# Moving small constants and two attention pools so that matmul operands start at multiples of 512 bytes

## The chip, the cores and the metric

The kernel runs on one core of a Trainium2 chip. The metric is the device time of one execution in microseconds (us). The core has five engines that work side by side: TensorE (PE) multiplies, and its weight loads (PEld) are recorded separately; VectorE (DVE) and ScalarE (ACT) do elementwise work; GpSimd (POOL) does elementwise work between SBUF tiles; SyncE (SP) issues nearly all DMA transfers. SBUF is the working memory of 128 partitions; a tile takes the same byte range in every partition, and its start address below is the byte at which that range begins. PSUM takes the results of the matmuls.

## The reference, cut to what matters

One encoder layer (depth 1, so only mixer A), in float32, on 2048 tokens of width 1024:

```python
mod = (silu(c) @ ada_w + ada_b); sh1, sc1, g1, sh2, sc2, g2 = split(mod, 6)
h = rmsnorm(x, mix_norm_pre) * (1 + sc1) + sh1
y = windowed_gqa_sink(h, w_qkv, w_o, sink, rel_bias)   # 16 heads, 4 KV heads, window +-128
x = x + g1 * rmsnorm(y, mix_norm_post)
h = rmsnorm(x, ffn_norm_pre) * (1 + sc2) + sh2
y = (silu(a) * b) @ w_out, where a, b = split(h @ w_in, 2)   # hidden 2816
x = x + g2 * rmsnorm(y, ffn_norm_post)
```

## The kernel before, in words

**Number format.** A float32 product is made of three matmuls on rounded parts: `three` (lines 147 to 151) multiplies high weights by high activations (L149), high weights by low activations (L150) and low weights by high activations (L151). `split` (line 153) makes the parts: ACT copies the rounded high part (L154), DVE or POOL subtracts it (L155). Nearly every matmul has a stationary operand (the weights) of 128 x 128 values, 512 bytes per partition, and a moving operand of 128 x 512 values, 2048 bytes per partition. Each matmul is preceded by a load of its weights, which goes on while the matmul before it still streams.

**Stages.** (1) The projections of token chunks 0 and 1 (`Chunk`, `w_piece`, `qkv_tile`; matmuls `psq<-hi,w` and `psv`). (2) Attention, 64 units of 128 queries and one KV head each (`Unit`): `scores` (L432), transposes of the probabilities (L455), `values` (L460, L461). Between the units a `Budget` puts filler matmuls on PE: the projections of chunks 2 and 3 (`psq<-hi,ws`), later the output projection of chunks 0 to 2 (`py<-ol,wo`). (3) The output projection of chunk 3 (`last_o`, again `py<-ol,wo`), once attention has given its memory back. (4) The first FFN product (`Hidden`, `pc_i`) in two halves of 1024 tokens: for each of 22 output tiles seven block products (`Block.STEPS`) of 12 matmuls each. (5) The second product (`Outs`, `pc_o`): in seven parts of m = 2 or 3 pairs of hidden tiles (`PARTS`), four blocks per part, each of seven steps of 3 x m matmuls. (6) A last part without the block scheme (`pl`), and the final norm.

**Order.** The instructions of an engine run in a fixed order, which a scheduler works out when the program is built. SP's DMA issues are one such queue: an issue that waits holds up all behind it.

**Where tiles lie.** Tiles live in pools, and pools are stacks that grow from both ends of SBUF: `side="left"` upwards, `side="right"` downwards. A pool opened later lies further in; a pool's memory is used again once it is closed, and a new tile then waits for the last users of the old ones (`reuse_waits="tile"`). Sizes are rounded up to 32 bytes. So one tile of an odd size moves every pool that is opened behind it on that side:

- Left: 1152 bytes are taken before the kernel's first tile. `const` (lines 106 to 113) adds 192 + 192 + 128 + 64 + 512 + 512 + 32 + 128 = 1760 bytes, so the next pool starts at 2912 = 5 x 512 + 352. All left pools behind it hold tiles whose sizes are multiples of 512: each operand there starts 352 bytes past a multiple of 512. `ones` and `ident`, inside `const`, start at 192 past one.
- Right: the end is at 229,344 = 447 x 512 + 480. All right pools with tiles of whole multiples of 512 give operands at 480 past a multiple.
- In attention `sm` (eight tiles of 32 bytes) and `pp` (three tiles `pr` of 6176 bytes) take 18,784 bytes = 36 x 512 + 352, so the pools opened after them, `ptp`, `ob` and `ws` (lines 376 to 378), hold operands at 128 past a multiple.

Which operand comes from which side, with its start past a multiple of 512 ("offset"):

| Matmuls | moving operand | weights |
|---|---|---|
| `psq<-hi,w`, `psq<-lo,w` (stage 1) | `hs`, left, 352 | `w1`, `w2`, right, 480 |
| `psq<-hi,ws` (fillers) | `hs`, left, 352 | `ws`, right, 128 |
| `py<-ol,wo`, chunks 0 to 2 | `op`, left, 352 | `ws`, right, 128 |
| `o<-phi,v`, `o<-plo,v` | `ptp`, right, 128 | `v` in `qkv`, right, 480 |
| `s<-k,q` | `k` in `qkv`, right, 480 | `q` in `qkv`, right, 480 |
| `py<-ol,wo`, chunk 3 | `op3`, right, 480 | `wop3`, right, 480 |
| `pc_i`, steps 0 to 4 of 7 | left, 352 | even tiles `wi0`, left, 352; odd tiles `wi1`, right, 480 |
| `pc_i`, steps 5 and 6 | `hB`, right, 480 | the same |
| `pc_o`, two steps (`hb11o`, `ht2o`) | `hA2`, left, 352 | `wo`, left, 352 |
| `pc_o`, the other five steps | `hB2`, right, 480 | `wo`, left, 352 |
| `pl<-gls,wl` | half left, 352; half right, 480 | `hB2`, right, 480 |

**The hand-over after attention.** When `att` closes (line 682), `yp3`, `wop3` and `op3` (lines 688 to 690) are opened on the right, over attention's memory. `OProj.fill` loads four tiles `ol` (attention's output, L543) and, per output tile, a raw weight `wor` (L553), which ACT and DVE split into `wo`.

Of the kernel before, what the change touches and what calls it, by code (L numbers as in the profile page):

```python
# [11 lines left out]
F32 = mybir.dt.float32  # L12
# [6 lines left out]
P = 128  # L19
S = 2048  # L20
D = 1024
KT = D // P
# [25 lines left out]
LAG = 2  # L48
# [15 lines left out]
def f(ap):  # L64
    return ap.bitcast(F32)
# [8 lines left out]
def encoder_layer(ctx, tc, a):  # L74
# [4 lines left out]
    def open_pool(stack, name, bufs=1, side="left", space=None):  # L79
        kw = {"space": space} if space is not None else {"side": side}  # L80
        return stack.enter_context(tc.tile_pool(name=name, bufs=bufs, reuse_waits="tile", **kw) if space is not DRAM
                                   else tc.tile_pool(name=name, bufs=bufs, space=DRAM))

    const = open_pool(ctx, "const")
    dram = open_pool(ctx, "dram", space=DRAM)

    q_d = [[dram.tile([P, GRP, CH], F32, name=f"q_d{c}_{g}") for g in range(KVH)] for c in range(NCH)]
# [15 lines left out]
    tab_d = dram.tile([HEADS, RLEN], F32, name="tab_d")  # L103


    mod = const.tile([P, 48], F32, name="mod")
    adab = const.tile([P, 48], F32, name="adab")
    gains = const.tile([P, 4, KT], F32, name="gains")
    nsink = const.tile([P, HEADS], F32, name="nsink")
    ones = const.tile([P, P], F32R, name="ones")  # L110
    ident = const.tile([P, P], F32, name="ident")
    epsc = const.tile([P, 1], F32, name="epsc")
    coef = const.tile([P, 4, KT], F32, name="coef")
    dve.memset(f(ones), 1.0 / D)
    dve.memset(epsc, EPS)
    make_identity(nc, ident)
# [254 lines left out]
    att = ExitStack()  # L371
    bp = open_pool(att, "bp", side="right")
    qkv = open_pool(att, "qkv", 2, side="right")
    sm = open_pool(att, "sm", 4, side="right")
    pp = open_pool(att, "pp", LAG + 1, side="right")
    ptp = open_pool(att, "ptp", 4, side="right")
    ob = open_pool(att, "ob", 2, side="right")
    wop = ws = open_pool(att, "ws", 2, side="right")
    psF = open_pool(ctx, "psF", 2, space=PSUM)
    psS = open_pool(att, "psS", 2, space=PSUM)  # L380
    psT = open_pool(att, "psT", 3, space=PSUM)
# [751 lines left out]
```

## Time and profile before

| | |
|---|---|
| Median of 3 runs | 2166.03 us (2165.94 to 2170.61) |
| The profiled execution, first to last instruction | 2164.3 us |
| Instructions in it | 28,995, of them 9366 matmuls |
| ACT busy | 1076.4 us (50%) |
| POOL busy | 737.5 us (34%) |
| DMA moved | 396.35 MB, mean 183 GB/s |

A row of a view of the trace reads: start in us from the span's start, duration in us, engine, source line, operation, tile written <- tiles read, shape, and in brackets the idle time of the engine before it with what ended it. The end of a matmul is modelled and overlaps the next one; the distance from one start to the next is what PE takes per matmul, and that is what is read below. Tile names have their numbers left out.

### The profile page before, as it was taken

The page shows a single profiled execution, that of the slowest core. Times are in us where ns is not written, and L with a number is a line of the kernel's source. Part 1 is how long each engine was busy: PE and PEld are TensorE (multiplying, and loading weights), DVE is VectorE, ACT ScalarE, POOL GpSimd, SP SyncE. Part 2 cuts the span into 40 slices and gives each one's busy share as a digit, 9 for nine tenths or more (in the row PEclk, how much of TensorE's full clock was granted, in tenths as well). Part 3 has the DMA queues.
Part 4 walks back from the last instruction along what each step waited for, and adds up shares of the span by engine and source line. Part 5 has one row for each costly group of instructions (what it writes and reads, how often), then busy time and mean ns, then how long its engine had stood idle before and what let it go on. Part 6 is the DMA issues. An engine that isn't in the chain of part 4 may idle for free. (4 is left out here: it accounts for less than half of the span.)

```text
span 2164.3 us, 28995 instructions
## 1 busy us (share of the span) xinstructions
PE 2055.8 (95%) x9366; PEld 1666.6 (77%) x9366; DVE 1649.8 (76%) x2933; ACT 1076.4 (50%) x2125; POOL 737.5 (34%) x687
## 2 busy tenths in 40 slices
PE   6898999989989989999999999999999999998996
PEld 4786877878867768878887877888888788877886
DVE  7656767665676669876878897767673888999987
ACT  4546666577777746343434342333332844465422
POOL 3404343367778723434344422222221000220030
PEclk8999999999999989999999999999999999999998
DMA  8877665576667695545455764332231644438442
GB/s 279 261 254 253 184 182 175 159 282 233 227 199 245 189 347 206 183 148 162 138 178 194 257 220 142 112 106 94 98 117 54 210 153 138 141 129 280 161 132 103
DMA packets 200516, 396.35 MB, mean 183 GB/s; under 512 B 20091, under 2 KB 62124, under 8 KB 195244
## 3 DMA queue, kind: packets, MB, share of 16 engines
q1 hardware_dynamic: 199788, 393.97, 54.7%
q8 instruction: 74, 1.21, 0.2%
q14 instruction: 78, 0.64, 0.1%
q10 hardware_dynamic: 576, 0.52, 0.1%
HBM read 270.65 MB, written 123.76 MB: 182 GB/s over the span
## 5 line engine op out<-in xcount | busy, mean ns | idle before, releaser
L437 DVE CUSTOM_DVE_ANT_0 pr<-s,bias,nsink 128x384 f32<-128x384 f32 (+1 forms) x256 | 149.3, 596 | 91.5 <-PE s L432 74.3
L149 PE MATMUL pc_i<-ht,ws_i 128*128 128x512 f32 x528 | 207.2, 393 | 2.1 <-DVE b_i L799 1.5
L150 PE MATMUL pc_i<-ht,ws_i 128*128 128x512 f32 x528 | 206.9, 392 | 0.0
L151 PE MATMUL pc_i<-ht,ws_i 128*128 128x512 f32 x528 | 206.9, 392 | 0.0
L439 ACT ACTIVATE pr<-pr,nm 128x385 f32<-128x385 f32 (+1 forms) x256 | 153.8, 603 | 71.3 <-DVE nm L437 64.3
L815 POOL TENSOR_TENSOR p_i<-p_i,u_i 128x512 f32<-128x512 f32 x44 | 71.5, 1625 | 310.7 <-DVE u_i L802 153.6
L445 POOL TENSOR_SCALAR pr<-pr,rs 128x384 f32<-128x384 f32 (+1 forms) x256 | 147.4, 601 | 83.0 <-DVE rs L443 82.9
L946 POOL TENSOR_TENSOR z<-z,z 128x512 f32<-128x512 f32 x32 | 52.5, 1654 | 359.2 <-DVE z L942 342.3
L432 PE MATMUL s<-k,q 128*128 128x384 f32 (+1 forms) x512 | 136.1, 359 | 20.2 <-DVE nm L437 13.6
L149 PE MATMUL pc_i<-hb,wa_i 128*128 128x512 f32 x352 | 139.1, 395 | 2.0 <-DVE u_i L789 2.0
L150 PE MATMUL pc_i<-hb,wa_i 128*128 128x512 f32 x352 | 138.7, 394 | 0.0
L151 PE MATMUL pc_i<-hb,wa_i 128*128 128x512 f32 x352 | 138.7, 394 | 0.0
L155 DVE TENSOR_TENSOR plo<-t,phi 128x512 fp32r<-128x512 f32 x184 | 121.7, 685 | 16.2 <-ACT phi L154 14.7
L154 ACT CAST wa_i<-wiri 128x512 fp32r<-128x512 f32 x132 | 81.8, 620 | 102.2 <-PE pc_i L151 94.7
L154 ACT CAST ws_i<-s_i 128x512 fp32r<-128x512 f32 x132 | 81.6, 618 | 102.5 <-PE pc_i L151 98.7
L432 PEld LDWEIGHTS s<-k,q 128*128 128x128 f32 x512 | 86.6, 193 | 44.9 <-DVE nm L437 27.8
L149 PEld LDWEIGHTS pc_i<-ht,ws_i 128*128 128x128 f32 x528 | 99.3, 188 | 25.5 <-DVE b_i L799 2.2
L151 PEld LDWEIGHTS pc_i<-ht,ws_i 128*128 128x128 f32 x528 | 99.2, 188 | 22.4
L150 PEld LDWEIGHTS pc_i<-ht,ws_i 128*128 128x128 f32 x528 | 99.2, 188 | 22.2
L455 PE MATMUL t<-ident,pr 128*128 128x128 f32 x736 | 113.1, 273 | 3.1 <-POOL pr L445 2.4
L149 PE MATMUL py<-ol,wo 128*128 128x512 f32 x256 | 103.3, 405 | 11.9 <-ACT wo L154 7.4
L155 DVE TENSOR_TENSOR ws_i<-s_i,ws_i 128x512 fp32r<-128x512 f32 x132 | 104.6, 792 | 10.9 <-ACT ws_i L154 10.7
(320 smaller groups left out, 6142.8 us busy)
## 6 DMA issues: line engine op xcount, KB each, us to landing
wiri<-w_in SPq DMA_DIRECT2D x88, 512.0 KB, 4.8
ada<-ada_w SPq DMA_DIRECT2D x40, 512.0 KB, 4.9
wiro<-w_out SPq DMA_DIRECT2D x48, 384.0 KB, 3.9
q_d<-e SPq DMA_DIRECT2D x64, 256.0 KB, 3.9
q<-q_d SPq DMA_DIRECT2D x16, 1024.0 KB, 5.8
wo<-wo_d SPq DMA_DIRECT2D x16, 1024.0 KB, 5.7
g_d_b<-p_i SPq DMA_DIRECT2D x44, 256.0 KB, 4.7
g_d_t<-p_i SPq DMA_DIRECT2D x40, 256.0 KB, 2.0
```

The lines of the kernel that those rows point to most:

```text
L149: pe.matmul(ps, w[0], h[0], start=first, stop=False)
L150: pe.matmul(ps, w[0], h[1], start=False, stop=False)
L151: pe.matmul(ps, w[1], h[0], start=False, stop=last)
L154: act.copy(hi, src)
L155: return eng.tensor_tensor(lo, src, f(hi), ALU.subtract).ins
L432: m = pe.matmul(ps[:, :n], q[:, h, jb * P:(jb + 1) * P], kk[:, i, (jb + j0) * P:(jb + j1) * P], start=i == 0, stop=i == 1)
L437: red = dve.tensor_tensor_reduce(pr[:, h, :n], ps[:, :n], bias[g][:, h, j0 * P:j1 * P], -1.0, nsink[:, hh:hh + 1], ALU.add, ALU.min, nm[:, ...
L439: act.activation(pr[:, h, :n + 1], pr[:, h, :n + 1], AF.Exp, bias=nm[:, h:h + 1], scale=-1.0, accum_out=rs[:, h:h + 1])
L445: pool.tensor_scalar(pr[:, h, :n], pr[:, h, :n], rs[:, h:h + 1], 1.0, ALU.mult, ALU.mult)
L455: pe.transpose(pt[:, h * P:(h + 1) * P], pr[:, h, jj * P:(jj + 1) * P], ident)
L815: pool.tensor_tensor(sa, sa, b, ALU.mult)
L946: (pool if (i, x) in ((2, 2), (4, 4), (5, 5), (6, 6)) else dve).tensor_tensor(sums[hf, n2, x], sums[hf, n2, x], sums[hf, n2, y], ALU.add)
```

## The change

It moves tiles and pools; it adds, removes and resizes no operation. `mod` is declared with 80 columns instead of 48, of which 48 are used as before. `adab`, `gains`, `epsc` and `coef` go to a new pool `constr` at the right end: 192 + 128 + 32 + 128 = 480 bytes, so the right pools now start at 228,864 = 447 x 512. On the left `const` is 320 + 64 + 512 + 512 = 1408 bytes; `ones` starts at 1536, `ident` at 2048 and the next pool at 2560, all multiples of 512. In attention `sm` and `pp` are opened last, behind `ptp`, `ob` and `ws`. The one matmul operand that stays off a multiple of 512 is `pr` in the transposes (L455), whose rows are 385 values wide.

```diff
     const = open_pool(ctx, "const")
+    constr = open_pool(ctx, "constr", side="right")
     dram = open_pool(ctx, "dram", space=DRAM)
...
-    mod = const.tile([P, 48], F32, name="mod")
-    adab = const.tile([P, 48], F32, name="adab")
-    gains = const.tile([P, 4, KT], F32, name="gains")
+    mod = const.tile([P, 80], F32, name="mod")
+    adab = constr.tile([P, 48], F32, name="adab")
+    gains = constr.tile([P, 4, KT], F32, name="gains")
     nsink = const.tile([P, HEADS], F32, name="nsink")
     ones = const.tile([P, P], F32R, name="ones")
     ident = const.tile([P, P], F32, name="ident")
-    epsc = const.tile([P, 1], F32, name="epsc")
-    coef = const.tile([P, 4, KT], F32, name="coef")
+    epsc = constr.tile([P, 1], F32, name="epsc")
+    coef = constr.tile([P, 4, KT], F32, name="coef")
...
     qkv = open_pool(att, "qkv", 2, side="right")
-    sm = open_pool(att, "sm", 4, side="right")
-    pp = open_pool(att, "pp", LAG + 1, side="right")
     ptp = open_pool(att, "ptp", 4, side="right")
     ob = open_pool(att, "ob", 2, side="right")
     wop = ws = open_pool(att, "ws", 2, side="right")
+    sm = open_pool(att, "sm", 4, side="right")
+    pp = open_pool(att, "pp", LAG + 1, side="right")
```

In the built program the order of instructions is the same on every engine up to the hand-over after attention. There SP's queue differs: before, it issues `ol` 0 early, then `ol` 1, `ol` 2, `wor` 0, `ol` 3, `wor` 1, `wor` 2; after, `wor` 0 takes the early place, then come `wor` 1, 2, 3 and behind them `ol` 0 to 3. Some instructions of ACT, DVE and PE in this stretch and in the first blocks of `pc_i` change places with it.

## The prediction

> **What bounds the kernel now.** I read the page first, then busy time by stage, then PE's waits.
>
> ```profile
> span 2164.3 us, 28995 instructions
> PE 2055.8 (95%) x9366; PEld 1666.6 (77%) x9366; DVE 1649.8 (76%) x2933; ACT 1076.4 (50%) x2125; POOL 737.5 (34%) x687
> PEclk8999999999999989999999999999999999999998
> ```
> ```profile
> 0.00:182.00 182.00, 150.13 (x684) 120.32 (x684) 118.26 (x179) 86.21 (x145) 47.22 (x34) 0.93 0.80 263
> 182.00:756.00 574.00, 545.67 (x2770) 443.02 (x2770) 385.80 (x991) 404.49 (x931) 341.50 (x430) 0.99 0.65 210
> 756.00:822.00 66.00, 55.18 (x221) 44.44 (x222) 44.41 (x56) 35.60 (x56) 17.42 (x9) 0.90 0.97 354
> 822.00:1690.00 868.00, 858.10 (x3709) 697.11 (x3708) 671.45 (x956) 321.49 (x547) 277.40 (x183) 1.00 0.44 148
> 1690.00:2098.00 408.00, 396.69 (x1678) 317.32 (x1677) 378.78 (x651) 210.52 (x411) 50.39 (x31) 0.98 0.51 169
> 2098.00:2164.00 66.00, 49.99 (x309) 44.37 (x307) 51.09 (x102) 18.11 (x38) 3.60 (x3) 0.91 0.32 108
> ```
>
> The columns are the stretch, its length, busy time of PE, PEld, DVE, ACT and POOL, granted clock, DMA share, GB/s. PE has work in 858 of 868 us of `pc_i`, 397 of 408 us of `pc_o` and 546 of 574 us of attention, mostly at full clock. A busy PE here is a queue of matmuls: what a stretch costs is their number times the distance between two starts. PE hardly waits:
>
> ```profile
> PE s L432 <- DVE nm L437: 13.3, 20, 2.0
> PE nstl L131 <- DVE nhil L129: 5.5, 2, 4.0
> PE pc_o L149 <- DVE z L942: 6.5, 1, 6.5
> PE psq L149 <- ACT hi L154: 12.5, 3, 8.5
> ```
>
> These are the longest waits of attention, of `pc_i`, of `pc_o` and of the projections (total us, times, longest). So the question is only whether addresses alter the distance between starts.
>
> **They do already.** Two neighbouring blocks of `pc_i`, an even and an odd output tile, same line numbers and shapes, first and last row of each run without a gap:
>
> ```profile
> 1610.91 0.39 PE L149 MATMUL pc_i<-hb,wa_i 128*128 128x512 f32 x1
> ...
> 1624.29 0.39 PE L151 MATMUL pc_i<-ht,ws_i 128*128 128x512 f32 x1
> 1624.52 0.40 PE L149 MATMUL pc_i<-ht,wa_i 128*128 128x512 f32 x1
> ...
> 1629.88 0.39 PE L151 MATMUL pc_i<-hb,ws_i 128*128 128x512 f32 x1
> 1630.11 0.40 PE L149 MATMUL pc_i<-hb,wa_i 128*128 128x512 f32 x1
> ...
> 1643.88 0.39 PE L151 MATMUL pc_i<-ht,ws_i 128*128 128x512 f32 x1
> 1644.10 0.39 PE L149 MATMUL pc_i<-ht,wa_i 128*128 128x512 f32 x1
> ...
> 1649.33 0.40 PE L151 MATMUL pc_i<-hb,ws_i 128*128 128x512 f32 x1
> ```
>
> The runs have 60, 24, 60 and 24 rows, so the distances are 13.38/59 = 226.8 ns (moving and weights both at offset 352), 5.36/23 = 233.0 (480 and 352), 13.77/59 = 233.4 (352 and 480), 5.23/23 = 227.4 (both 480). Equal offsets: 227. Unequal: 233. The output projection shows it under one name, chunk 2 (352 and 128) and chunk 3 (both 480):
>
> ```profile
> 763.80 0.40 PE L149 MATMUL py<-ol,wo 128*128 128x512 f32 x1
> ...
> 766.37 0.40 PE L151 MATMUL py<-ol,wo 128*128 128x512 f32 x1
> ...
> 784.53 0.39 PE L150 MATMUL py<-ol,wo 128*128 128x512 f32 x1
> ...
> 797.45 0.39 PE L150 MATMUL py<-ol,wo 128*128 128x512 f32 x1
> ```
>
> 11 steps in 2.57 us are 233.6 ns, 57 in 12.92 are 226.7. Equal offsets also lie on the same side of SBUF in these cases; this pair separates the two:
>
> ```profile
> 633.17 0.40 PE L460 MATMUL o<-phi,v 128*128 128x512 f32 x1
> ...
> 634.34 0.39 PE L461 MATMUL o<-plo,v 128*128 128x512 f32 x1
> ```
>
> Both operands are on the right, at 128 and 480, and 5 steps take 1.17 us: 234 ns. So I take the offset past a multiple of 512, compared between the two operands, as what counts; the change makes it equal (zero) everywhere but in the transposes.
>
> **The change part by part.** Nothing is added or removed; each of the unequal matmuls should lose 233.3 - 227.1 = 6.2 ns.
>
> - Projections: 2 chunks x 10 tiles x 24 = 480 matmuls, 3.0 us on paper. This stage is also held by loads and splits (the 12.5 us wait above, DMA 0.80, clock 0.93), so between 0 and 3.0; I take 1.4.
> - Attention: 576 `psq<-hi,ws`, 576 `py` of chunks 0 to 2 and 368 of L460 and L461 are 1520, 9.4 us. PE is the fullest engine, but units pass through DVE, ACT and POOL too (the 13.3 us). If those set the pace nothing is won, if PE does all 9.4; 546 of 574 us busy is nearer the second: 7.9.
> - Hand-over: `wor` 1 to 3 now stand ahead of `ol` 0. Before:
>
> ```profile
> 774.15 0.80 PE L149 MATMUL py<-ol,wo 128*128 128x512 f32 x1 [7.38 <-ACT wo L154]
> ```
> ```profile
> 770.48 1.04 ACT L154 CAST ol<-ol 128x1024 fp32r<-128x1024 f32 x1 [2.50 <-DMA ol<-o_d]
> 771.77 1.04 ACT L154 CAST ol<-ol 128x1024 fp32r<-128x1024 f32 x1 [0.24 <-DMA ol<-o_d]
> 773.06 1.04 ACT L154 CAST wo<-wor 128x1024 fp32r<-128x1024 f32 x1 [0.24 <-DMA wor<-w_o]
> ```
> ```profile
> 760.00:780.00 20.00, 12.58 (x36) 9.17 (x35) 9.46 (x10) 7.02 (x8) 2.01 (x2) 0.67 1.02 375
> ```
>
>   Transfers of 512 KB land 1.29 us apart with the DMA engines full (1.02). PE waited for the third of them, `wor` 0. Now it waits for the fourth, `ol` 0; `ol` 1 to 3 follow it, each worth 6 matmuls of 0.43 us at the low clock. That is 1.3 us later; if every `ol` came late too, 4; if the earlier `wo` pays it back, 0. I take 1.3. Behind them on SP wait only `wiri` and stores that are due one landing later.
> - `pc_i`: 22 even tiles x 24 + 22 odd x 60 = 1848, 11.5 us; PE has nothing else to wait for but some 10 us: 10.9. Bounds 8 and 11.5.
> - `pc_o`: 5 of 7 steps, 28 blocks of 21 m, m = 2 in 4 of them, else 3: 1200 matmuls.
>
> ```profile
> 2068.77 0.39 PE L149 MATMUL pc_o<-hb11o,wa_o 128*128 128x512 f32 x1
> ...
> 2076.73 0.39 PE L151 MATMUL pc_o<-ht2o,ws_o 128*128 128x512 f32 x1
> 2076.95 0.40 PE L149 MATMUL pc_o<-hb21o,wa_o 128*128 128x512 f32 x1
> ...
> 2097.72 0.39 PE L151 MATMUL pc_o<-hb22o,ws_o 128*128 128x512 f32 x1
> ```
>
>   7.96/35 = 227.4 against 20.77/89 = 233.4: 6.0 ns, 7.2 us. But DVE fills part of this stage:
>
> ```profile
> 1840.00:1890.00 50.00, 50.00 (x218) 40.55 (x217) 50.00 (x82) 23.60 (x45) 12.51 (x8) 1.00 0.38 125
> 1890.00:1940.00 50.00, 47.71 (x189) 35.59 (x188) 50.00 (x79) 29.19 (x59) 15.87 (x8) 0.97 0.45 150
> 1940.00:1990.00 50.00, 43.49 (x180) 34.85 (x180) 49.67 (x89) 32.28 (x64) 0.00 (x0) 0.93 0.80 274
> ```
>
>   In 150 of 408 us a faster PE only waits for DVE sooner. 258/408 of 7.2 are 4.6. Bounds 2 and 7.2.
> - `pl`: 48 unequal matmuls, 0.3.
> - The 80 columns of `mod`, the constants' new side and the new place of `sm` and `pp` cost nothing: the same instructions read them, and the tiles under the new pools (`w1`) are done before attention starts. DVE and ACT tiles all move too; I count nothing for that.
>
> Sum: 1.4 + 7.9 - 1.3 + 10.9 + 4.6 + 0.3 = 23.8 us. The profiled execution's 2164.3 become 2140.5; the runs' median is 1.7 above that execution, so 2166.0 becomes 2142.
>
> A rule speaks against all of it. The Trainium skill, "TensorE: Matmul & The Clock Gate", section "Step-by-step: what each phase is for", says that PE reads the moving operand and the weights through two independent SBUF ports, and that loading the next weights takes no bandwidth from the running matmul. By that the sum would be zero, 2166. The trace disagrees: the same shapes with the same loads differ by 6 ns with the addresses.
>
> **The rivals.**
>
> *A, the offset itself costs too.* Equal offsets were only seen at 352 and 480. If starting off a multiple of 512 has a price of its own, 227 falls further. The shortest long matmuls of this trace are of another kind (float32, 256 columns):
>
> ```profile
> 2144.96 3.62 PE L126 MATMUL nstz<-zsl,ones 128*128 128x256 f32 x16
> ```
>
> 16 in 3.62 us, about 0.216 apart once the last one's end is set aside. With 216 for all: 2568 equal matmuls of 512 columns x 11 ns = 28 us and 5096 x 17.3 ns = 88 us; at the same share (23.8 of 31.6 us, three quarters), 87 us: 2079. Against it: 352 and 480 give the same 227, and one operand at 128 beside the other at 352 or 480 gains nothing. The same page of the Trainium skill, section "Back-to-back issue gap", has 216 ns as the warm gap at 512 columns; no equal or unequal run here reaches it.
>
> *B, it does nothing.* If side or distance decides and not the offset, pairs from opposite sides stay at 233 and only the hand-over's 1.3 us is left: 2167. For it, most pairs read above confound the two; against it, `phi` and `v`. The rule of the two ports, from the Trainium skill's page named above, would come to this time as well.
>
> *C, slower: zero is a bad phase.* If loads and streams that begin at the same multiple of 512 get in each other's way, the 2568 matmuls that take 227 now go to 233: 2568 x 6.2 = 16 us, with the hand-over 2183. It decides as soon as an aligned pair takes more than about 231 ns (where 5096 gains of 2.3 and 2568 losses of 4 cancel). For it: no pair at zero was seen. Against it: two different equal offsets behave alike.
>
> **How the numbers follow.** Forecast 0.79; A, in full or in part, 0.11; B 0.05; C 0.05. About 0.3% (6.5 us) is what runs of this kernel can tell from no change, so faster 0.90, same 0.05, slower 0.05. The range starts at 2110, part of A (the full paper sum of 31.6 us is 2134), and ends at 2156, where attention gives nothing and the FFN terms are at their lower bounds: 1.4 - 1.3 + 8 + 2 is 10.
>
> **What would show it.** Distances of 227 ns in odd blocks of `pc_i` and in `py` of chunks 0 to 2, where 233 stood; the even blocks unchanged. `pc_i` as a stage shorter by about 11 us; `pc_o` by less than its matmuls save, with DVE still full; `py`'s first wait of chunk 3 ended by `ol` and about 1.3 us longer. Distances still at 233 make B, at 233 in all blocks C, near 216 A. If the distances are 227 and the total still falls by less than 10 us, my shares for attention and `pc_o` are wrong.

## The result, and the profile after

| | before | changed |
|---|---|---|
| Median | 2168.32 us (2165.94 to 2170.99, 4 runs) | 2156.39 us (2153.88 to 2159.60, 4 runs) |
| Ratio of the two | | 0.9947, 95% interval 0.9931 to 0.9962 |
| Profiled execution, first to last instruction | 2164.3 us | 2155.7 us |

Faster by 11.9 us, half of the 23.8 us of the forecast, 0.4 us outside the range. The page of the changed kernel, the lines that answer to those of before:

```profile
span 2155.7 us, 29001 instructions
PE 2037.4 (95%) x9366; PEld 1669.6 (77%) x9366; DVE 1648.5 (76%) x2933; ACT 1076.0 (50%) x2125; POOL 735.7 (34%) x687
PEclk9998999999999989999999999999999999999998
```

PE works 18.4 us less, 2055.8 to 2037.4, and the span is only 8.6 us shorter: the rest has become waiting. Busy time by stretch of the changed kernel, columns as before and the same stretches, in which its own stages begin 2 to 8 us earlier:

```profile
182.00:756.00 574.00, 544.53 (x2769) 446.28 (x2768) 390.20 (x994) 406.50 (x934) 342.11 (x431) 0.98 0.64 210
756.00:822.00 66.00, 56.87 (x222) 44.73 (x222) 45.07 (x55) 35.13 (x56) 11.10 (x8) 0.88 0.93 333
822.00:1690.00 868.00, 848.01 (x3712) 696.32 (x3710) 670.79 (x957) 322.97 (x547) 280.71 (x183) 1.00 0.44 149
```

In `pc_i` PE falls from 858.1 to 848.0 of the same 868 us, which is nearly the 10.9 us of the forecast, but the stage moves by 2. In attention PE's busy time hardly falls at all (545.7 to 544.5). An odd block of `pc_i` in the changed kernel, first and last row of the 60 matmuls that were 233.4 ns apart, and of the 24 that were 227.4:

```profile
1628.58 0.39 PE L150 MATMUL pc_i<-hb,wa_i 128*128 128x512 f32 x1
...
1641.95 0.39 PE L152 MATMUL pc_i<-ht,ws_i 128*128 128x512 f32 x1
1642.17 0.39 PE L150 MATMUL pc_i<-ht,wa_i 128*128 128x512 f32 x1
...
1647.39 0.39 PE L152 MATMUL pc_i<-hb,ws_i 128*128 128x512 f32 x1
```

13.37/59 = 226.6 and 5.22/23 = 227.0 ns: the distances are as forecast. A block of 84 matmuls that nothing disturbs goes from 19.20 (even) and 19.46 us (odd) to 19.04, start to start. What took the place of the saved time is in PE's waits from 815 to 1690 us (engine, line and tile, what it waited for; total us, times, longest), the changed kernel:

```profile
PE nstl L132 <- DVE nhil L130: 6.8, 2, 5.0
PE pc_i L150 <- ACT p_i L787: 4.0, 2, 2.9
PE pc_i L150 <- DVE b_i L800: 3.3, 3, 1.7
PE pc_i L150 <- DVE u_i L790: 3.2, 4, 1.3
```

17.3 us together. The kernel before has 9.2 for the same four: 5.5 for `nstl`, as shown in the prediction, and these:

```profile
PE pc_i L149 <- DVE u_i L789: 2.0, 2, 1.7
PE pc_i L149 <- DVE b_i L799: 1.5, 1, 1.5
PE pc_i L149 <- ACT p_i L786: 0.2, 1, 0.2
```

The hand-over, first `py` of chunk 3 on PE, then ACT, changed kernel:

```profile
772.16 1.22 PE L150 MATMUL py<-ol,wo 128*128 128x512 f32 x2 [8.04 <-ACT ol L155]
```
```profile
766.47 1.04 ACT L155 CAST wo<-wor 128x1024 fp32r<-128x1024 f32 x1 [1.14 <-DMA wor<-w_o]
771.07 2.00 ACT L155 CAST ol<-ol 128x1024 fp32r<-128x1024 f32 x2 [3.55 <-DMA ol<-o_d]
773.78 1.04 ACT L155 CAST ol<-ol 128x1024 fp32r<-128x1024 f32 x1 [0.71 <-DMA ol<-o_d]
```

`wor` is there early and PE now waits for `ol`, 8.04 us in place of 7.38, as forecast in kind.

Distances between marks on PE show where time goes. The marks are the starts of the 480 projection matmuls (first to last), of the 1st and 257th `s`, of the 577th `py` (the first of chunk 3), of the 85th, 1849th, 2354th and last of the 3696 `pc_i`, of the first `pc_o` and of the first `pl`. `pc_i` has 44 blocks of 84; the halves change in blocks 20 to 26. Four further kernels of the experiments stand beside, all from profiled executions:

| us | before | changed | order only | equal, old order | stores on ACT, unequal | stores on ACT, equal |
|---|---|---|---|---|---|---|
| projections | 153.6 | 150.3 | 152.1 | 152.1 | 152.0 | 150.5 |
| attention, first half | 280.1 | 278.7 | 281.9 | 279.8 | 280.3 | 277.7 |
| attention, second half | 310.4 | 312.4 | 312.0 | 311.2 | 311.2 | 311.2 |
| chunk 3's `py`, `pc_i` block 0 | 66.1 | 67.7 | 67.3 | 64.6 | 65.6 | 65.1 |
| `pc_i` blocks 1 to 21 | 416.8 | 417.2 | 418.3 | 416.9 | 409.9 | 407.2 |
| the next 505 `pc_i`, about blocks 22 to 27 | 122.2 | 124.2 | 124.6 | 124.2 | 122.7 | 125.0 |
| the last 1342 `pc_i` | 308.8 | 304.2 | 308.8 | 304.2 | 308.8 | 304.2 |
| `pc_o` | 409.7 | 403.9 | 407.9 | 404.4 | 411.3 | 404.1 |
| span | 2164.3 | 2155.7 | 2169.1 | 2153.5 | 2157.3 | 2142.8 |

The last 1342 of `pc_i` gain all that their distances promise, 4.6 us. Blocks 1 to 21 gain nothing in sum, and not because each of them stands still: blocks 7 to 15 and 17 to 20 wait for nothing and fall from 252.0 to 248.0 us, again what their distances promise. In the changed kernel blocks 1 to 6 grow by 2.4 (124.0 to 126.5), block 16 by 0.2 and block 21 by 1.8. With equal offsets and the old order they grow by 1.5, 1.9 and 0.6.

### The profile page after: what moved, and what is told of

Same layout as the page of the kernel before. It is cut to its first block, busy times and chain, and to the rows that moved or that the text cites. A ratio compares the mean times of both kernels' runs of the same rounds, so it can differ in the third digit from the quotient of the medians.

```text
span 2155.7 us, 29001 instructions
## 1 busy us (share of the span) xinstructions
PE 2037.4 (95%) x9366; PEld 1669.6 (77%) x9366; DVE 1648.5 (76%) x2933; ACT 1076.0 (50%) x2125; POOL 735.7 (34%) x687
## 5 line engine op out<-in xcount | busy, mean ns | idle before, releaser
L440 ACT ACTIVATE pr<-pr,nm 128x385 f32<-128x385 f32 (+1 forms) x256 | 153.8, 603 | 70.7 <-DVE nm L438 65.3
L156 DVE TENSOR_TENSOR wa_i<-wiri,wa_i 128x512 fp32r<-128x512 f32 x132 | 109.1, 826 | 5.1 <-ACT wa_i L155 4.9
```

The costliest lines, as they stand in the source:

```text
L156: return eng.tensor_tensor(lo, src, f(hi), ALU.subtract).ins
L440: act.activation(pr[:, h, :n + 1], pr[:, h, :n + 1], AF.Exp, bias=nm[:, h:h + 1], scale=-1.0, accum_out=rs[:, h:h + 1])
```

## The experiments

**Equal, but not at zero; and the order alone.** Three kernels share the runs of the kernel before (2166.82 us, 11 runs). `mod` wider, nothing else:

```diff
-    mod = const.tile([P, 48], F32, name="mod")
+    mod = const.tile([P, 80], F32, name="mod")
```

> The kernel before with `mod` 32 columns wider and nothing else: weights and moving operands of projections, `pc_i`, `pc_o` and `pl` then all lie at 480 bytes past a multiple of 512, while the attention's fillers (480 against 128) and `o` (128 against 480) stay unequal; every engine's order, the loads after the attention among it, is the one of before.
> Mechanism. If the two offsets need only be equal, all distances in `pc_i` and `pc_o` are 227 ns and those in the attention 231 to 233, as before. If the operands must lie at a multiple of 512 itself, they stay at 233 and the time at 2168 us.
> Where the missing half went. R1 (the time saved is waited for again: the attention is paced by its unit's chain and not by TensorE, and the `pc_i` blocks 4 to 6 and 20 to 25 by chains of VectorE, GpSimd and loads of a fixed length): projections -3.4, attention 0 to -1, hand-over 0, `pc_i` -3 to -6, `pc_o` -6, in all about 2155 us (2151 to 2158). R2 (the loads after the attention, put in another order, delay everything behind them, and that ate the gain of `pc_i`): the order is the old one here, so `pc_i` keeps about 11, in all about 2147 us (2144 to 2150).

Measured: 2154.86 us, ratio 0.9944 (0.9927 to 0.9960). All `pc_i` and `pc_o` distances are 227 at 480 and 480; `psq` and `py` that stayed unequal have 233.5. So equality counts and zero does not. (The 256-column matmuls `psv` of stage 1, one operand on each side like `psq`, gain nothing: 118.7 ns before, 119.7 here.) The time is R1's.

```diff
-    sm = open_pool(att, "sm", 4, side="right")
-    pp = open_pool(att, "pp", LAG + 1, side="right")
     ptp = open_pool(att, "ptp", 4, side="right")
...
     wop = ws = open_pool(att, "ws", 2, side="right")
+    sm = open_pool(att, "sm", 4, side="right")
+    pp = open_pool(att, "pp", LAG + 1, side="right")
```

> The kernel before with the pools `sm` and `pp` opened last and nothing else: the loads after the attention come in the changed kernel's order on every engine; the offsets of projections, `pc_i`, `pc_o` and `pl` stay as before (352 or 480), the attention's fillers stay unequal, only `o` has equal ones (480 and 480).
> R1: the other order costs what the marks of the two traces show at chunk 3's `py`, 2 to 4 us at the first `pc_i` block, and the rest of the kernel takes that up in part: 2167 to 2171 us. R2: the delay is passed on and grows behind: 2173 to 2180 us, with `pc_i` some 8 us longer than before.

Measured: 2171.94 us, ratio 1.0026 (1.0013 to 1.0039). The other order costs about 5 us with these offsets, between the two expectations: 2.6 are there when `pc_i`'s second block starts, the rest is added in blocks 1 to 27 (418.3 and 124.6 in the table).

```diff
-    mod = const.tile([P, 48], F32, name="mod")
+    mod = const.tile([P, 80], F32, name="mod")
...
     sm = open_pool(att, "sm", 4, side="right")
+    sm.tile([P, 40], F32, tag="pad", name="pad", bufs=1)
```

> The kernel before with `mod` 32 columns wider and a tile of 160 bytes beside those of `sm`, the pools in their old places: every 512-column matmul has both operands 480 bytes past a multiple of 512, in the attention too, and every engine's order is the one of before.
> Both theories of the mechanism as in the run with `mod` alone. R1: as that run, with the attention 1 to 2 us shorter: 2154 us (2150 to 2157); `pc_i` saves 3 to 6 of 11.5 and the waits `nstl` behind `nhil` in its blocks 5 and 21 are as long as in the changed kernel (6.8 us together). R2: `pc_i` keeps its 11, in all 2146 us (2143 to 2149), and those waits are as in the kernel before (5.5).

Measured: 2155.40 us, ratio 0.9946 (0.9929 to 0.9963). With the old order and every offset equal, blocks 1 to 21 still take 416.9 us and the time is that of the changed kernel. R2 falls: the delay at the hand-over is real, but it isn't what ate `pc_i`'s gain. Nor does making the attention's operands equal (this run against the one with `mod` alone) show in the time.

**What is the grain?**

```diff
-    mod = const.tile([P, 80], F32, name="mod")
+    mod = const.tile([P, 144], F32, name="mod")
```

> The changed kernel with `mod` 64 columns wider than it makes it: the left side's operands lie 256 bytes past a multiple of 512, the right side's at 0; order as in the changed kernel.
> If operands must agree modulo 512, the undisturbed `pc_i` blocks of 84 matmuls are 19.20 (even) and 19.46 us (odd) again, as before, and the time is that of the run with the order alone, 2172 us (2168 to 2176). If they need only agree modulo 256 or less, all blocks stay at 19.04 and the time at 2156.

Measured in a single run: 2158.16 us. The same odd block, first and last row of its 84, left operands at 256 and right ones at 0:

```profile
1629.21 0.39 PE L150 MATMUL pc_i<-hb,wa_i 128*128 128x512 f32 x1
...
1648.03 0.39 PE L152 MATMUL pc_i<-hb,ws_i 128*128 128x512 f32 x1
```

18.82/83 = 226.7 ns: a difference of 256 is no difference. 128 (480 and 352, before) is one, so of the grains tried the operands must agree modulo 256.

```diff
-    mod = const.tile([P, 80], F32, name="mod")
+    mod = const.tile([P, 88], F32, name="mod")
```

> The changed kernel with `mod` 8 columns wider than it makes it: the left side's operands lie 32 bytes past a multiple of 512, the right side's at 0; order as in the changed kernel.
> If every difference costs, `pc_i` blocks of 19.20 and 19.46 us and 2172 us (2168 to 2176), as with a difference of 128 or 256 bytes. If only a difference past some grain of the memory costs (64 bytes or more), blocks of 19.04 us and 2156. Anything between would show a cost that grows with the difference.

Measured in a single run: 2178.99 us. The same odd block with a difference of 32, the 60 unequal matmuls and then the 24 equal ones:

```profile
1641.42 0.39 PE L150 MATMUL pc_i<-hb,wa_i 128*128 128x512 f32 x1
...
1655.19 0.39 PE L152 MATMUL pc_i<-ht,ws_i 128*128 128x512 f32 x1
1655.42 0.40 PE L150 MATMUL pc_i<-ht,wa_i 128*128 128x512 f32 x1
...
1660.67 0.40 PE L152 MATMUL pc_i<-hb,ws_i 128*128 128x512 f32 x1
```

13.77/59 = 233.4 and 5.25/23 = 228.3: 32 bytes cost as much as 128. The 7 us above the run with the order alone are not explained by the distances (blocks of 19.23 and 19.48); with a single run they stay open.

**Moving the work that PE waits for.** The longest wait in `pc_i` is the matmul of a statistic behind its last residuals. One `yield` moved, in the changed kernel:

```diff
             rstd_of(temp, psF, "mm", acc, f"lo{c}", r)
...
-            yield
...
+            yield
             r = temp(f"lr2{c}", "r", 2)
             rstd_of(temp, psF, "mm", acc, f"l{c}", r)
```

> The changed kernel with one `yield` of `late_residuals` moved from behind the first rstd to ahead of the second: the first residual's work is given out one step earlier and the second statistic one step later, the number of steps is the same.
> R1: the waits of `nstl` behind `nhil` (6.8 us in the changed kernel, 5.0 the longest at 945.6) change with it, by 2 us or more, and the time with them: 2152 to 2155 us if they shorten. R2: those waits are not what ate the gain; the time stays at 2156 us within 1.5 whatever they do.

and, on the kernel with equal offsets and the old order, the residuals in three steps:

```diff
-                if k % 2:
+                if k in (2, 5, 7):
                     yield
+            yield
             r = temp(f"lr2{c}", "r", 2)
```

> The kernel with all offsets equal and the old order (`mod` wider, the 160-byte tile in `sm`), and in `late_residuals` the eight residuals given out over three steps (0 to 2, 3 to 5, 6 and 7) in place of four, and an empty step ahead of the second statistic; 20 steps as before, the first residual not moved ahead.
> R1: the `nstl` waits behind `nhil` (6.9 us in the run with equal offsets and old order) go away, and the wait behind `p_i` that moving the first residual ahead brought (6.2 us in block 1) does not come, so `pc_i` is 4 to 7 us shorter than there: 2149 us (2146 to 2153). R2 (and any theory in which these waits are not what takes the gain back): 2155 us within 2.

Measured: 2153.73 us, 0.9943 (0.9921 to 0.9964), and 2156.66 us, 0.9942 (0.9925 to 0.9959). PE's waits in blocks 1 to 21, first the kernel with equal offsets and old order, then the two in turn:

```profile
PE nstl L131 <- DVE nhil L129: 6.9, 2, 5.0
PE pc_i L149 <- ACT p_i L787: 1.5, 1, 1.5
```
```profile
PE pc_i L150 <- ACT p_i L787: 7.3, 2, 6.2
PE pc_i L150 <- DVE b_i L800: 1.1, 1, 1.1
```
```profile
PE pc_i L149 <- ACT p_i L787: 8.9, 4, 4.0
```

The `nstl` wait went as meant, and a wait for ACT took its place: in ACT's queue the copy of `pc_i`'s first product stands behind a square of the late residuals. In the first of the two, one profile has blocks 1 to 21 at 413.0 us, but the time can't be told from that of the changed kernel; the second, for which R1 expected 2149, has them at 416.7. So taking away one wait does not free the stretch: the same late work is met at another place.

```diff
     def late_ada():
+        for i in range(4):
+            yield
         for i in range(2):
```

> The same kernel with equal offsets and the old order, with four empty steps ahead of `late_ada`'s first one, so that its reductions on VectorE begin four blocks of `pc_i` later, behind the change of halves.
> R1 with VectorE as what holds blocks 20 to 25: these blocks, 127.4 us of 120 to 121.6 undisturbed in the run without the empty steps (blocks 20 to 25: 19.04, 20.05, 23.51, 21.14, 19.96, 21.11, of which some is other matmuls' time), become 2 to 5 us shorter: 2151 us (2149 to 2154). If loads or the `b` operands of the second half hold them, nothing changes: 2155 within 2.

Measured: 2153.46 us, 0.9930 (0.9905 to 0.9955), which can't be told from 2155.40. Blocks 20 to 25 took 126.6 us, and without the empty steps 124.8 (the six numbers in the expectation add up to this, not to 127.4): longer, so `late_ada` isn't what holds them. Two stretches at the change of halves, first without, then with the empty steps (same columns as the stretches above):

```profile
1255.00:1275.00 20.00, 17.65 (x75) 13.37 (x73) 20.00 (x28) 10.06 (x18) 7.67 (x5) 1.00 0.83 285
1275.00:1295.00 20.00, 17.82 (x76) 13.84 (x75) 20.00 (x34) 6.62 (x12) 4.23 (x3) 1.00 0.38 129
```
```profile
1255.00:1275.00 20.00, 17.39 (x73) 12.86 (x71) 20.00 (x28) 9.92 (x19) 7.98 (x5) 1.00 0.83 290
1275.00:1295.00 20.00, 16.78 (x63) 12.78 (x64) 20.00 (x34) 6.62 (x12) 3.50 (x3) 0.91 0.36 126
```

DVE has 20.00 of 20 us in all four rows: here it is full with other work, and a faster PE only waits.

```diff
                 residual(c, k, y, temp(f"lx{c}_{k}"), r, acc, temp)
-                if k % 2:
-                    yield
+                yield
+            yield
+            yield
...
                 yield
+                yield
...
                 sp.dma_start(w, a["ada_w"][t][:, cols])
+                yield
                 yield
...
             for i in range(7):
                 hid.step(i)
-            next(late, None)
+                if i in (2, 6):
+                    next(late, None)
```

> The kernel with equal offsets and the old order, with the late work given out in steps of half the size, two in each `pc_i` block (behind its third and its last product): one residual a step, two empty steps ahead of the second statistic, every step of the second norm's application and of `late_ada` followed by an empty one; so each block has the same work as before but for the statistic's place, in smaller pieces.
> R1 as it stands after the runs that moved a step (the chain of late work that TensorE or ScalarE's queue meets has to be taken up somewhere; a wait removed in one block comes back in another when a step grows): with smaller steps the waits behind `nhil` and `p_i` together fall under 4 us in blocks 1 to 19 (6.9 + 1.5 in the run with equal offsets and old order, 8.9 in the run with the statistic later), and the time to 2149 us (2146 to 2153). If the waits come from loads that are late whatever the size of a step, they stay at 7 to 9 us, and the time at 2155 within 2.

Measured: 2169.90 us, 1.0012 (0.9999 to 1.0025): both expectations missed. Blocks 1 to 21 took 430.8 us; the waits behind `nhil` stayed (6.2 us) and new ones behind DVE's drains of products came (7.0 us). Late work put between a block's products seems to delay the drains behind it. Smaller steps aren't the remedy.

**Is it the attention's transposes?** In the changed kernel the fillers of attention have equal offsets, yet average 229.1 ns. One place, PE's rows, changed kernel:

```profile
654.44 0.82 PE L456 MATMUL t<-ident,pr 128*128 128x128 f32 x6
655.01 0.48 PE L150 MATMUL py<-ol,wo 128*128 128x512 f32 x1
655.33 0.39 PE L151 MATMUL py<-ol,wo 128*128 128x512 f32 x1
...
656.94 0.39 PE L152 MATMUL py<-ol,wo 128*128 128x512 f32 x1
...
659.89 0.39 PE L150 MATMUL py<-ol,wo 128*128 128x512 f32 x1
```

The first step behind the transposes takes 0.32 us, the next 7 take 1.61 (230 each), the 13 after that 2.95 (226.9).

```diff
             ps = psC.tile([P, CH], F32, tag="p", name=f"pc{i}_{self.u}")
+            for g in range(GRP):
+                pe.transpose(ps[:, g * P:(g + 1) * P], ident, ident)
             for k in range(m):
```

> The changed kernel with four 128x128 transposes of `ident` ahead of every product of the feed-forward, into the first tile that the product then overwrites: some 360 groups of four at about 109 ns, 150 to 160 us more.
> In the attention the first eight or so 512-column matmuls behind a run of transposes lie 228 to 232 ns apart although their offsets are equal, and only later ones 227. If the short matmuls do that, the first eight distances of each `pc_i` product (12 matmuls) are at 228 to 232 here too, where they are 227 in the changed kernel; if it is the attention's other work (its loads, or reads and writes of the other engines), they stay at 227 from the first or second on.

Measured in a single run: 2351.13 us, 195 more (there are 504 groups, not 360). A product in it:

```profile
1738.26 0.60 PE L761 MATMUL pc_i<-ident 128*128 128x128 f32 x4
1738.62 0.48 PE L150 MATMUL pc_i<-hb,wa_i 128*128 128x512 f32 x1
1738.94 0.39 PE L151 MATMUL pc_i<-hb,wa_i 128*128 128x512 f32 x1
...
1740.32 0.39 PE L151 MATMUL pc_i<-hb,wa_i 128*128 128x512 f32 x1
1741.23 0.39 PE L152 MATMUL pc_i<-hb,wa_i 128*128 128x512 f32 x1
```

Again 0.32, then 6 steps in 1.38 us (230), then 4 in 0.91 (227.5). The means over some 298 products by position are 232.8, 234.6, 232.1, 228.3, 230.8, 231.3, then 227.5 to 229.6, and 226.7 from the tenth. The same stage without transposes has 226.8 throughout, so these transposes do it; whether by their 128 columns, by being float32 in place of float32r or by being transposes was not varied. `ident` lies at equal offsets with itself, so it isn't the odd start of `pr`.

**What paces blocks 1 to 21.** With the offsets as before or equal, in the old order or the new, they take 416 to 418 us, though the undisturbed blocks among them gain. What does not come sooner is the start of the statistics of the late residuals (`nstl`), in blocks 6 and 16. Counted from the start of block 1, the first starts after 102.6 us and the second after 300.8 before, 105.7 and 300.9 in the changed kernel, 103.8 and 300.1 with equal offsets in the old order. A PE that gets there sooner only waits longer. Block 16, before and with equal offsets in the old order:

```profile
1141.05 0.50 PE L131 MATMUL nstl<-nhil,ones 128*128 128x512 f32 x1 [1.44 <-DVE nhil L129]
```
```profile
1137.70 0.50 PE L131 MATMUL nstl<-nhil,ones 128*128 128x512 f32 x1 [1.92 <-DVE nhil L129]
```

The longer wait cost more than its own 0.5 us. From 1141.00 to 1145.00 us before, the granted clock was 1.00. From 1137.70 to 1142.00 in the other kernel it was 0.60, and seven steps took 427 ns each. Behind the longer waits of block 6 steps of 427 ns stand in all three kernels.

The residuals are loaded and stored through SP's DMA queue, so its own waits belong here too. SP issues nearly all loads and stores in order, and the largest item from 840 to 1240 us is a store of late residuals (`x1_d`) that waits for DVE to finish the tile; first before, then the changed kernel:

```profile
SPq L509 <- DVE ly L508: 83.5, 15, 10.1
```
```profile
SPq L510 <- DVE ly L509: 84.0, 15, 9.9
```

Behind it stand the next loads. The 16 stores moved to ACT's queue, once with equal offsets and the old order, once with the offsets of before; these two kernels have the same order on every engine:

```diff
-    def residual(c, k, y, xr, r, acc, alloc, eng=dve):
+    def residual(c, k, y, xr, r, acc, alloc, eng=dve, late=False):
...
-        sp.dma_start(x1_d[c][:, k, :], y)
+        if not late:
+            sp.dma_start(x1_d[c][:, k, :], y)
...
             act.activation(sq, y, AF.Square)
             pool.tensor_tensor(acc, acc, sq, ALU.add)
+        if late:
+            act.dma_start(x1_d[c][:, k, :], y)
...
-                residual(c, k, y, temp(f"lx{c}_{k}"), r, acc, temp)
+                residual(c, k, y, temp(f"lx{c}_{k}"), r, acc, temp, late=True)
```

> The kernel with equal offsets and the old order, with the 16 stores of the late residuals (`x1_d`) issued from ScalarE's queue, behind the square that reads the same tile, in place of SP's queue, where they waited 83.3 us of the 400 from 840 to 1240 for VectorE's `ly` with all later loads behind them.
> From `pc_i`'s matmul 85 to 1849 the kernels take 416.8 us (before), 417.2 (changed) and 416.9 (equal offsets, old order), whatever a matmul's distance is. R3 (SP's queue in order, stores that wait with loads behind them, sets the pace of blocks 1 to 21): the stretch falls to 405 to 413 and the time to 2148 us (2143 to 2152). R4 (VectorE's, GpSimd's and the loads' own work sets it, SP only waits for them): the stretch stays at 416 to 418 and the time at 2155 within 2.

> The kernel before with the same 16 stores on ScalarE's queue; offsets as before (352, 480, 128), every engine's order that of the run with these stores and equal offsets.
> R3: the pair of kernels with the stores on ScalarE's queue shows what equal offsets are worth where SP's queue holds TensorE less: 15 to 20 us between them in place of 11.4, of which 4 to 7 between `pc_i`'s matmul 85 and 1849 (0 without the move). So this kernel is at 2160 to 2167 us. R4: 10 to 13 us between them, 0 to 2 in that stretch, and this kernel at 2166 within 2.

Measured: 2144.57 us, 0.9889 (0.9875 to 0.9902), with equal offsets, and 2159.54 us, 0.9961 (0.9946 to 0.9975), with those of before (2168.79, 11 runs). SP's wait for `ly`, the equal one and the unequal one:

```profile
SPq L507 <- DVE ly L509: 12.0, 3, 6.7
```
```profile
SPq L506 <- DVE ly L508: 11.7, 3, 7.0
```

Blocks 1 to 21 fall to 407.2 and 409.9 us, and the two statistics now start 100.0 and 293.2 us (equal) and 99.7 and 294.0 us (unequal) after block 1: earlier than before by 3 and 7 us, and nearly the same for both distances of the matmuls. How the queue does it shows in block 5. Before, the next tile's load leaves SP 0.37 us behind the store, for which SP had waited some 6 us; with the stores on ACT's queue it follows at once on the load ahead of it, here with the offsets of before:

```profile
925.68 0.32 SPq L509 DMA_DIRECT2D x_d<-ly  x1
926.05 0.42 SPq L840 DMA_DIRECT2D ly<-y_d  x1
```
```profile
916.04 0.40 SPq L506 DMA_DIRECT2D lx<-xT  x1
916.48 0.43 SPq L843 DMA_DIRECT2D ly<-y_d  x1
```

SP itself waits little less for that: with equal offsets its waits from 840 to 1240 us add up to 303 us in place of 312, because others grow (for `wa_i` from 79.0 to 86.7). What counts is what stands behind a wait.

R3 holds in the stretch and, but for 0.5 us in the second, in the time; the first of the two is faster than the changed kernel and the one before. Equal offsets are worth 15.0 us between the two medians, at the lower end of what R3 said; but the runs of the second spread from 2155.78 to 2165.50, so this isn't told from the 11.4 to 12 without the move. The stretch gives 2.6 of it, less than the 4 to 7 expected: block 6 still waits for its statistic, 2.5 us in the first and 1.6 in the second.

The stores kept on SP's queue, but issued a step later, and the changed kernel with the stores on ACT's queue:

```diff
+            held = []
             for k in range(KT):
...
+                held.append((k, y))
                 if k % 2:
                     yield
+                    for kk, yy in held:
+                        sp.dma_start(x1_d[c][:, kk, :], yy)
+                    held = []
```

> The kernel with equal offsets and the old order, with the 16 stores of the late residuals kept on SP's queue but issued at the beginning of the next step, a `pc_i` block later, when VectorE has long written the tile; the tile is held a block longer.
> R3 (in the queue, the stores' wait with later loads behind it is the cost): the 83.3 us that SP's queue waited for `ly` fall under 30, the stretch from `pc_i`'s matmul 85 to 1849 falls from 416.9 to 406 to 412, and the time to 2148 us (2143 to 2151), near the 2144.6 of the stores on ScalarE's queue. R5 (the move to ScalarE's queue helped because a second queue moves more, or because a tile was given back sooner): the stretch stays at 415 to 419, the time at 2155 within 2.

> The changed kernel with the same 16 stores on ScalarE's queue; otherwise unchanged, with its own order of the loads after the attention.
> If the other order costs TensorE only at the hand-over, this kernel is 2 to 4 us behind the 2144.6 of the old order with the same stores: 2147 us (2145 to 2150), `pc_i`'s first block begins 2 to 3 us later and the rest takes as long. If SP's queue had absorbed it in blocks 1 to 21, the difference shows only now; if the order costs nothing once that queue is free, 2144 to 2145.

Measured: 2152.98 us, 0.9943 (0.9924 to 0.9962), and 2149.26 us, 0.9911 (0.9886 to 0.9937). The first doesn't decide, because the wait that it should remove stayed, a row of the deferred stores' kernel:

```profile
SPq L849 <- DVE ly L509: 77.1, 14, 10.5
```

SP seems to run more than a step ahead of DVE. Blocks 1 to 21 took 416.0 us there and 409.6 in the second, where the wait is 12.4. So the stretch is short (407 to 410) in the three kernels in which SP's wait is 12 us, and 416 to 417 with 77 to 84 (before, changed, equal offsets in the old order, and with the deferred stores). Where late work was moved the wait was 57 to 71 and the stretch 413 to 431, so it isn't the only thing that counts there; and that the second queue also helped in another way is not excluded. The changed order is 4.7 us behind the old one with the same stores, of which 1.6 are there at `pc_i`'s second block; but the intervals overlap, and one of its four runs took 2140.70.

## Why the prediction was half right

- **The mechanism** was right: equal offsets give 227, unequal 233, at 0, 256, 352 and 480 alike. The grain was read too coarse: pairs modulo 512 were all that the trace showed, and 256 suffices. Rivals A (an offset has a price of its own), B (it does nothing) and C (zero is bad) are out. The rule of two independent ports from the Trainium skill, "TensorE: Matmul & The Clock Gate", section "Step-by-step: what each phase is for", would have both at one distance; the runs disagree (226.7 and 233.4 with 32 bytes moved).
- **`pc_i`, the step that failed most**: "PE has nothing else to wait for but some 10 us: 10.9. Bounds 8 and 11.5." The matmuls saved 10.1 us of PE's time and the stage 2.2. The step that failed: the waits of some 10 us were left at their length, so that PE, busy 858 of 868 us, would set the pace everywhere else. But a wait ends when other work is done, and a PE that comes sooner waits longer. In blocks 1 to 21 the late residuals, whose loads stand behind stores in SP's queue, set when the statistics can start. The undisturbed blocks gained 4.0, and longer waits, some with a lower clock behind them, took it back (0 gained). At the change of halves, where DVE is full, the changed kernel lost 2.0, and so did the kernel with equal offsets and the old order. Only the last 1342 matmuls gained and kept it, 4.6. With the stores off SP's queue equal offsets bring 4.9 in `pc_i` from block 1 on.
- **Attention, the second**: "546 of 574 us busy is nearer the second: 7.9." Mean over five profiles with unequal fillers against ten with equal ones: first half 280.97 to 278.68, second half 311.98 to 311.85, so 2.4 us; the first halves overlap by 0.1 only (280.05 to 281.92 and 277.07 to 280.13). Without the run with a difference of 32, whose second half is the longest, it is 1.7. One cause is shown: behind transposes the gain sets in only after some eight matmuls. Fillers go from 233 to 229.1, not 227, and neighbouring `o` from 233.9 to 230.5, so the 9.4 us on paper were nearer 6 (an estimate: 1152 x 4 and 368 x 3.4 ns). That the rest goes into waits of the units' chain was not tested by itself.
- **Hand-over**: -1.3 was taken. From chunk 3's first `py` to `pc_i`'s second block six kernels of the changed order take 67.6 us and nine of the old one 65.3: 2.3. With what follows from it the order costs 5.1 us by itself and 4.7 with the stores on ACT's queue, though only 1.0 between the changed kernel and equal offsets in the old order. The intervals overlap in the last two pairs, so only the first is clear of noise.
- **Projections** 1.4: 1.8 between the means of four unequal profiles and eleven equal ones (152.5 and 150.7); the changed kernel's own was 3.3. **`pc_o`** 4.6: 5.8, within its bounds of 2 to 7.2; 7.2 in the pair with the stores on ACT's queue. Its reason held too: parts 4 to 6 of the seven, where DVE is full, gain 0.2 us together, the second, third and last 1.25 each, the first 1.9. **`pl`** 0.3: 0.26.
- The last sentence of the prediction looked for the fault, should the gain stay under 10 us, in attention and `pc_o`. It was 11.9, and the fault was in attention and `pc_i`.

## What to carry to other kernels

Give moving operand and weights the same address modulo 256 bytes; here a pad of 160 bytes and a wider constant do it, without the new order of pools, which cost 5 us by itself with unequal offsets. An engine that is 99% busy can still be held: before a gain per instruction is multiplied by their number, ask of each of its waits what ends it, and whether that comes sooner when the engine is faster. Read the waits of the other queues in that stage for it, SP's included. Then compare the stage block by block: here the blocks without a wait kept their gain, and the few with one took it back.

## What was not expected of the hardware

A 512-column float32r matmul is 6 ns dearer on average when the offsets of its two operands differ modulo 256 by as little as 32 bytes, with both operands on the right of SBUF (`o`, 233.9 ns) or one on each side. At 256 columns it isn't: `psv` has 118.4 to 119.1 ns in three kernels with unequal offsets and 119.7 to 119.8 in four with equal ones. Whether the matmul's own weights count, or the next one's, which load while it streams, was not told apart; their offsets are the same within a block. After four 128x128 float32 transposes the next step takes 0.32 us and some eight more take 228 to 235 ns before they settle at 227; with unequal offsets no such settling is seen, the fillers of the kernel before are at 231 to 234 at every position behind the first.
